# Weight sums of a seven-product matrix multiplication, formed in another order

## The chip, the core and the metric

The kernel runs on one core of one Trainium2 chip. The metric is device time in microseconds (us), from launch to end, taken as the median of several runs. The engines of a core run side by side, each in its own program order, and wait for one another through semaphores: PE is TensorE (its weight loads are listed as PEld), DVE is VectorE, ACT is ScalarE, POOL is GpSimd and SP is SyncE, which here issues the loads. A DMA that adds to its destination is issued on POOL.

## The reference

Two layers of a block over 528 tokens (16 meta tokens, 512 inputs) of width 1024, all in fp32. Each layer projects the normalized input with one wide matrix `w_in`, runs a sparse attention and a pooling branch, and mixes both under gates:

```
proj = jnp.einsum('btd,de->bte', h, w_in)
q, k, v, gate_a, u_b, gate_b, q_idx, k_idx, w_idx, merge = jnp.split(proj, ...)
...
attn = indexer_sparse_attention(q, k, v, q_idx, k_idx, w_idx, k_top)   # top 128 keys of a query
y_a = jnp.einsum('bte,ed->btd', attn * jax.nn.silu(gate_a), w_a)
y_b = jnp.einsum('bte,ed->btd', pooled * jax.nn.silu(gate_b), w_b)
g_a, g_b = jnp.split(jax.nn.sigmoid(merge), 2, axis=-1)
return x + jnp.einsum('btd,de->bte', g_a * y_a + g_b * y_b, w_out)
```

The change concerns the columns of `w_in` for `gate_a` (512) and `merge` (2048): ten chunks of 256 columns in each layer.

## The kernel before

**Precision.** A product in fp32 is made of three fast matmuls: each operand is split into a high part (a cast, on ACT) and a low part (operand less high part, on DVE), and high*high, high*low and low*high are added up in PSUM.

**Seven products.** For these ten chunks the 1024 x 256 weight block and the activations are cut into 2 x 2 quarters, and the four quarter results come from seven products instead of eight (Winograd's form of Strassen's method). A product is 12 matmuls of 128x128 weights on 264 columns in layer 0 and 256 in layer 1. The weight operands are the quarters a11, a12, a22 and four sums: s3 = a11 + a21, s1 = a21 + a22, s2 = s3 + a22, s4 = a12 + s2. The activations' sums are formed earlier, once in a layer.

**A group** (one round `q` of the loop in `mix_gates`) is the work of one chunk: seven products into three PSUM banks U, S and X. U gathers several products, and in between partial results are read out of it: `out` copies a bank on ACT (rows `p` and `u`), and `total` adds a bank and such a copy on DVE (rows `c<-d,p`, `c<-d,u`, and `sila<-d,p`, `sila<-d,u` in the first two groups of a layer). `gate` then takes a tanh on ACT. Banks change roles from group to group: the next group's U is this one's X, its X this one's S, its S this one's U. The order before is a11 into U, a12 into X, s2 into U, s1 into S, s3 into U, s4 into S, a22 into U.

**Where the weights come from.** A chunk's two `raw` tiles (four quarters in all) are loaded by SP, two chunks in flight; `w_load` asks for the next chunk once a chunk's last low part is taken. `mixed_prep` forms the operands in nine items, i0 to i8: casts on ACT (`hi`, L244), subtractions on DVE (`lo`, rows `w<-raw,w`), two sums on DVE (rows `s<-raw` and `raw<-s,raw`) and two sums by accumulating DMA issued on POOL (L253 for s1, L263 for s4). At each product's end the loop takes items so that some five of the next chunk's nine are done when its group begins; in the program's order i0 and i1 of the next chunk stand behind a group's fourth product, i2 behind the fifth, i3 and i4 behind the sixth and seventh, and the rest in its own group behind the first three. `NEEDS` says which item a product must have behind it.

**What runs beside it.** After each product `group_done` lets a step of the attention (`logits`, `soft`, `scale`, `turn`, `values`) be emitted, so that PE has matmuls of the attention between some products. In the first groups of a layer DVE also does the top-k rounds (`MAX8`, `MATCH_REPLACE8`). PE and DVE run in the order in which the program emits; the instructions of ACT, POOL and SP are placed by the framework's scheduler. PSUM has three `d` banks for U, S, X, four `a` banks and one `v` bank for the attention. POOL further scales the meta keys (`pm`, L765).

Of the kernel before, what the change touches and what calls it, by code (L numbers as in the profile page):

```python
# [8 lines left out]
F32 = mybir.dt.float32  # L9
F32R = mybir.dt.float32r  # L10
AF = mybir.ActivationFunctionType
OP = mybir.AluOpType
# [16 lines left out]
LB = 6  # L29
# [60 lines left out]
def tile_block(ctx: ExitStack, tc: tile.TileContext, x, meta, w_in, pool_w, w_a, w_b, w_out, rows, hgain, c_tab, out):  # L90
# [42 lines left out]
    raws, ready = {}, {}  # L133
# [37 lines left out]
    def w_prep_enqueue(casts_first=False, after=None):  # L171
        c = W["prep"]
        if c >= len(chunks):
            return
        W["prep"] += 1
        kt = chunks[c][0][0].shape[1]
        cols = 2048 // kt
        if c in plain:
            return
        ready[c] = {}  # L180
        if c in mixed:
            prep_q.extend(mixed_prep(c))
            return
        parts = ready[c] = ([], [])

        def split(which):
            t = w_tile().rearrange("p (k e) -> p k e", e=cols)
            parts[which].extend(t[:, k] for k in range(kt // 2))
            return t

        his = {}

        def high(s):
            his[s] = split(0)
            act.copy(his[s], raws[c][s])

        def low(s):
            dve.tensor_sub(split(1), raws[c][s], f(his[s]))
            if s == 1:
                del raws[c]  # L200
                w_load()

        def second():
            low(0)
            high(1)

        def minus(s):
            t = split(1)
            act.activation(t, raws[c][s], AF.Copy, scale=-1.0)  # L209
            gp.dma_start(t, raws[c][s], accum_op=OP.add)  # L210

        def plus(s):
            t = split(0)
            act.copy(t, raws[c][s])
            if s == 1:
                del raws[c]
                w_load()

        def highs():
            with tc.issue_after(after) if after else nullcontext():  # L220
                high(0)
                high(1)

        if casts_first:
            prep_q.extend((highs, lambda: low(0), lambda: low(1)))
        elif c in by_dma:
            prep_q.extend((lambda: minus(0), lambda: minus(1), lambda: plus(0)))
            if c in metas:
                prep_q.append(lambda: meta_queries(metas[c], raws[c]))
            prep_q.append(lambda: plus(1))  # L230
        else:
            prep_q.extend((lambda: high(0), second, lambda: low(1)))

    def mixed_prep(c):

        r0, r1 = raws[c]
        blk = {"a11": r0[:, 0], "a21": r0[:, 1], "a12": r1[:, 0], "a22": r1[:, 1]}
        src = {"a11": "a11", "a12": "a12", "a22": "a22", "s3": "s3", "s2": "a11", "s1": "a21", "s4": "a12"}
        ops = ready[c]

        def hi(n):
            t = w_tile().rearrange("p (s k e) -> p s k e", s=2, k=4)
            ops[n] = t
            act.copy(t[:, 0], blk[src[n]])  # L244

        def lo(n):
            dve.tensor_sub(ops[n][:, 1], blk[src[n]], f(ops[n][:, 0]))

        def i0():
            blk["s3"] = tmp.tile([128, 544], F32, tag="L", name="s3", bufs=LB)[:, :512].rearrange(  # L250
                "p (k e) -> p k e", k=4)
            dve.tensor_add(blk["s3"], blk["a11"], blk["a21"])
            gp.dma_start(blk["a21"], blk["a22"], accum_op=OP.add)  # L253
            hi("a11")

        def i1():
            lo("a11")
            dve.tensor_add(blk["a11"], blk["s3"], blk["a22"])
            hi("a12")

        def i2():
            lo("a12")
            gp.dma_start(blk["a12"], blk["a11"], accum_op=OP.add)  # L263

        def i3():
            hi("s2")

        def i4():
            lo("s2")
            hi("s1")  # L270

        def i5():
            lo("s1")
            hi("s3")

        def i6():
            lo("s3")
            hi("s4")

        def i7():  # L280
            lo("s4")
            hi("a22")

        def i8():
            lo("a22")
            del raws[c]
            w_load()

        def counted(fn):
            def item():  # L290
                fn()
                progress[c] += 1
            return item

        progress[c] = 0
        return [counted(fn) for fn in (i0, i1, i2, i3, i4, i5, i6, i7, i8)]
# [643 lines left out]
        return early, late, last_sum, operands  # L940

    ROLES = [(0, 1, 2), (2, 0, 1), (1, 2, 0)]
    NEEDS = {"a11": 1, "a12": 2, "s2": 4, "s1": 5, "s3": 6, "s4": 7, "a22": 8}

    def mix_gates(sa, zb, ta, s0, n2, operands, splits, alos):
        base = popped[0] - progress[W["use"]]
        for q in range(-2, 8):
            c = W["use"]
            W["use"] += 1
            ops = ready[c]  # L950
            w_prep_enqueue()
            bs = [bank("d") for _ in range(3)]
            U, S, X = (bs[r] for r in ROLES[(q + 2) % 3])
            done = [0]

            def product(ps, name, start):
                while progress[c] <= NEEDS[name]:
                    prep_one()
                B, wt = operands[name], ops[name]
                for k in range(4):  # L960
                    for e, (x, y) in enumerate(((0, 0), (0, 1), (1, 0))):
                        pe.matmul(ps[:, :n2], wt[:, x, k], B(y, k), start=start and k == e == 0,
                                  stop=k == 3 and e == 2, skip_group_check=True)

            def end():
                done[0] += 1
                group_done()
                while prep_q and (popped[0] < base + 9 * (q + 2) + LEAD + done[0] * 9 // 7 or (q == 7 and done[0] > 4)):
                    prep_one()

            def gate(eh, t, src, in_sheet):
                j = 2 * q + eh
                sign = -1.0 if eh else 1.0
                cs = slice(s0 + t * n2, s0 + (t + 1) * n2)
                if q < 0:
                    th = sheet(n2, "th")[:, :n2]
                    act.activation(th, src, AF.Tanh, scale=0.5)
                    d = sa[:, j + 4, cs]
                    later(lambda: dve.scalar_tensor_tensor(d, th, sign, src, op0=OP.add, op1=OP.mult),
                          3 if in_sheet else 2)  # L980
                elif q < 4:
                    th = src if in_sheet else sheet(n2, "th")[:, :n2]
                    act.activation(th, src, AF.Tanh, scale=0.5 * sign)
                    d = zb[:, j, cs]
                    later(lambda: dve.scalar_tensor_tensor(d, th, 1.0, d, op0=OP.add, op1=OP.mult), 2)
                else:
                    act.activation(ta[j - KT][:, cs], src, AF.Tanh, scale=0.5 * sign)

            def total(eh, t, ps, part):
                cs = slice(s0 + t * n2, s0 + (t + 1) * n2)  # L990
                o = sa[:, 2 * q + eh + 4, cs] if q < 0 else sheet(n2, "c")[:, :n2]
                dve.tensor_tensor(o, ps[:, :n2], part, op=OP.add)
                gate(eh, t, o, True)

            def out(ps, name):
                o = sheet(n2, name)[:, :n2]
                act.copy(o, ps[:, :n2])  # L997
                return o

            if q >= 4:  # L1000
                for j in (2 * q - KT, 2 * q + 1 - KT):
                    ta[j] = tmp.tile([128, T], F32, tag="B", name="ta", bufs=8)
            product(U, "a11", True)
            p1 = out(U, "p1")
            end()
            product(X, "a12", True)
            end()
            product(U, "s2", False)
            u = out(U, "u2")
            total(0, 0, X, p1)  # L1010
            end()
            product(S, "s1", True)
            p5 = out(S, "p5")
            end()
            if q == 7:
                alos()
            product(U, "s3", False)
            total(1, 1, U, p5)
            end()
            product(S, "s4", False)  # L1020
            end()
            product(U, "a22", False)
            total(0, 1, S, u)
            gate(1, 0, U[:, :n2], False)
            end()
            splits()
            ready.pop(c)
            if q == -1:
                later(lambda: SIL.update(ready=True), 4)
# [388 lines left out]
```

## Time and profile before

| what | value |
|---|---|
| median of 3 runs | 764.48 us (764.06 to 765.5) |
| profiled execution | 762.6 us |
| its span, first to last instruction | 760.7 us |
| PE busy | 738.2 us |
| DVE busy | 569.7 us |
| ACT busy | 474.9 us |
| POOL busy | 238.4 us |

The profiled execution is a run of its own, 1.9 us under the median; about 1.9 us of it lie outside the span. A row of the timeline reads: start in us from the span's start, duration, engine, line, operation, output<-inputs, shapes, count, and in brackets the engine's idle time before it and what ended it. All calls through the `Metered` wrapper, so all of PE's and DVE's, carry its line, L61; they are told apart by their tiles. A row of the waits reads: engine, what waited, what it waited for, us in total, times, longest. Where a group of rows is summed, the busy time and the mean duration in ns stand behind the bar, then the idle time before them. Matmuls are pipelined, so the end of a row overlaps the start of the next.

### The profile page before, as it was taken

The numbers are of one execution on the slowest core, as the hardware profiler recorded it, in microseconds if no ns is written. First come the engines' busy times: TensorE is split into PE (matmuls) and PEld (weight loads), VectorE is DVE, ScalarE is ACT, GpSimd is POOL, SyncE is SP. The second block draws the span as 40 slices with busy tenths as digits, with TensorE's granted clock in tenths as the row PEclk, the third lists the DMA queues.
The fourth block names the chain that finished last, engine by engine and source line by source line (L and its number), as shares of the span: only waits on it lengthen the run. The fifth ranks groups of instructions, "written<-read, shape, count | busy, mean of one in ns | idle before, by whom it ended". The sixth has DMA issues, their size and how long they took to land.

```text
span 760.7 us, 15982 instructions
## 1 busy us (share of the span) xinstructions
PE 738.2 (97%) x5962; PEld 708.9 (93%) x5962; DVE 569.7 (75%) x1436; ACT 474.9 (62%) x1077; POOL 238.4 (31%) x312
## 2 busy tenths in 40 slices
PE   8999999998999899999999999999999999999998
PEld 7999998998898899999998989998789999999998
DVE  6866998999886775794448668999989777658531
ACT  6669645656786887543245796557468778864320
POOL 3741075611122121063347411754023231205200
PEclk9999999999999999999999999999999999999999
DMA  7767755934454345443422676669255545346411
GB/s 259 226 166 169 167 126 123 239 99 99 113 124 97 92 103 126 140 161 134 141 85 84 165 180 175 165 155 228 41 141 115 128 94 125 85 130 206 139 43 42
DMA packets 99277, 103.26 MB, mean 136 GB/s; under 512 B 4816, under 2 KB 80368, under 8 KB 99200
## 3 DMA queue, kind: packets, MB, share of 16 engines
q1 hardware_dynamic: 88752, 74.89, 32.2%
q0 software_dynamic: 10368, 27.27, 19.4%
q8 instruction: 47, 0.77, 0.4%
q14 instruction: 30, 0.25, 0.1%
q10 hardware_dynamic: 80, 0.08, 0.0%
HBM read 66.41 MB, written 8.55 MB: 99 GB/s over the span
## 4 chain that ended last, share of the span: by engine, by line
PE 62%; DVE 19%; ACT 9%; DMA 6%; issue 3%; POOL 1%; DVEq 0%; SPq 0%; ACTq 0%; POOLq 0%
PE d L61 52%; PE a L61 8%; DMA raw<-raw 5%; DVE sc L61 4%; DVE m L61 3%; DVE w L61 3%; ACT w L244 3%; ACT lt L753 2%; DVE t L61 2%; PE v L61 2%; DVE qs L61 1%; ACT lt L764 1%; DVE ss L61 1%; DMA xt<-in_x_dram 1%; ACT pt L780 1%
## 5 line engine op out<-in xcount | busy, mean ns | idle before, releaser
L61 PE MATMUL d<-hhi,w 128*128 128x256 f32 (+3 forms) x1344 | 268.8, 292 | 0.5 <-DVE sila L61 0.3
L61 PEld LDWEIGHTS d<-hhi,w 128*128 128x128 f32 x1344 | 214.8, 189 | 3.8 <-issue 0.6
L61 PE MATMUL d<-hlo,w 128*128 128x256 f32 (+3 forms) x672 | 183.2, 289 | 0.0
L61 PEld LDWEIGHTS d<-hlo,w 128*128 128x128 f32 x672 | 126.8, 189 | 1.4 <-issue 0.2
L61 DVE TENSOR_TENSOR w<-raw,w 128x512 fp32r<-128x512 f32 (+1 forms) x152 | 124.5, 829 | 4.0 <-ACT w L244 3.9
L61 PE MATMUL d<-w,hhi 128*128 128x256 f32 x768 | 122.4, 288 | 0.8 <-DVE w L61 0.5
L61 PEld LDWEIGHTS d<-w,hhi 128*128 128x128 f32 x768 | 104.5, 189 | 5.2 <-issue 1.3
L61 PE MATMUL d<-hsum,w 128*128 128x264 f32 (+1 forms) x720 | 98.5, 289 | 7.8 <-ACT p L997 4.5
L61 PEld LDWEIGHTS d<-hsum,w 128*128 128x128 f32 x720 | 91.0, 191 | 10.4 <-ACT p L997 5.7
L244 ACT CAST w<-raw 128x512 fp32r<-128x512 f32 x120 | 70.8, 620 | 40.8 <-DVE raw L61 20.9
L61 PE MATMUL d<-w,hlo 128*128 128x256 f32 x384 | 72.3, 281 | 0.0
L61 PEld LDWEIGHTS d<-w,hlo 128*128 128x128 f32 x384 | 57.0, 188 | 0.0
L765 POOL TENSOR_SCALAR pm<-lt,rs 128x16 f32<-128x16 f32 x48 | 24.6, 558 | 98.3 <-DVE rs L61 89.0
L61 DVE MATCH_REPLACE8 sc<-m,sc 128x400 f32<-128x400 f32 (+2 forms) x100 | 54.3, 548 | 0.0
L61 DVE MAX8 m<-sc 128x8 f32<-128x400 f32 (+2 forms) x100 | 52.7, 556 | 0.9
L210 POOL DMA_DIRECT2D w<-raw x32 | 29.5, 940 | 72.5 <-ACT w L209 50.0
L61 PE MATMUL d<-mhi,w 128*128 128x272 f32 (+2 forms) x192 | 45.3, 324 | 0.0
L61 DVE SCALAR_TENSOR_TENSOR sc<-r,wsg,sc 128x144 f32<-128x144 f32 (+3 forms) x56 | 32.3, 581 | 16.1 <-ACT r L677 13.6
L753 ACT ACTIVATE lt<-lt,mn,NR 128x144 f32<-128x144 f32 (+3 forms) x64 | 42.3, 663 | 2.0 <-DVE mn L61 1.6
L253 POOL DMA_DIRECT2D raw<-raw x20 | 17.8, 889 | 79.3 <-DVE s L61 74.9
L1279 POOL TENSOR_TENSOR hlo<-ta,hhi 128x256 fp32r<-128x256 f32 (+1 forms) x28 | 28.3, 1021 | 43.3 <-PE d L61 30.5
L640 POOL TENSOR_TENSOR t<-t,t 128x256 f32<-128x256 f32 (+1 forms) x34 | 30.8, 907 | 26.8 <-DVE t L61 26.5
(215 smaller groups left out, 1442.4 us busy)
## 6 DMA issues: line engine op xcount, KB each, us to landing
raw<-in_w_in_dram SPq DMA_DIRECT2D x88, 256.0 KB, 3.1
raw<-in_w_in_dram SPq DMA_DIRECT2D x32, 512.0 KB, 4.6
w<-raw POOLq DMA_DIRECT2D x32, 512.0 KB, 5.3
raw<-raw POOLq DMA_DIRECT2D x40, 256.0 KB, 3.2
raw<-in_w_out_dram SPq DMA_DIRECT2D x16, 512.0 KB, 3.4
kept<-res SPq DMA_DIRECT2D x16, 264.0 KB, 4.8
res<-kept SPq DMA_DIRECT2D x16, 264.0 KB, 5.5
raw<-in_w_branch_b_dram SPq DMA_DIRECT2D x8, 512.0 KB, 5.0
```

Source lines behind the costliest of these rows:

```text
L61: return fn(*a, **k)
L210: gp.dma_start(t, raws[c][s], accum_op=OP.add)
L244: act.copy(t[:, 0], blk[src[n]])
L253: gp.dma_start(blk["a21"], blk["a22"], accum_op=OP.add)
L640: gp.tensor_tensor(t1[:m, :256], t1[:m, :256], t2[:m, :256], op=OP.add)
L753: act.activation(L[hh][:, :n], L[hh][:, :n], AF.Exp, scale=NR[:, i, h:h + 1], bias=mn[:, hh:hh + 1], accum_out=sm[:, hh:hh + 1])
L764: act.activation(L[hh][:, 16:n], L[hh][:, 16:n], AF.Copy, scale=rs[:, hh:hh + 1])
L765: (gp if j < 3 else dve).tensor_scalar(pms[i][:, 2 * j + hh, :], L[hh][:, 0:16], rs[:, hh:hh + 1], None, op0=OP.mult)
L780: act.copy(pt[:, :2 * len(bs)], tp[:, :256 * len(bs)].rearrange("p (a c) -> p a c", c=128))
L1279: pool_end = gp.tensor_sub(hlo[:, j, a:a + n], d, f(hhi[:, j, a:a + n]))
```

## The change

The sums are formed otherwise. s3 = a21 + a11 is now made by the accumulating DMA, in a21's place, by `first_sum`, which is called half a group ahead: in item i4 of the chunk before (for a layer's first chunk, at the end of the preparation before it). s2 = s3 + a22 is made on DVE in item i1, in a tile of its own. s4 = a12 + s2 stays a DMA in item i2. s1 = s2 - a11 is made on DVE, in a11's place, also in item i2. The last two products change places: a22 into U now comes right behind s3 into U, and s4 into S is the last; their operands are prepared in that order too, and the tanh of U stands behind a22, ahead of s4.

```diff
             if s == 1:
                 del raws[c]
                 w_load()
+                first_sum(c + 1)
...
+    def first_sum(c):
+        if c in mixed:
+            gp.dma_start(raws[c][0][:, 1], raws[c][0][:, 0], accum_op=OP.add)
+
...
-        src = {"a11": "a11", "a12": "a12", "a22": "a22", "s3": "s3", "s2": "a11", "s1": "a21", "s4": "a12"}
+        src = {"a11": "a11", "a12": "a12", "a22": "a22", "s3": "a21", "s2": "s2", "s1": "a11", "s4": "a12"}
...
         def i0():
-            blk["s3"] = tmp.tile([128, 544], F32, tag="L", name="s3", bufs=LB)[:, :512].rearrange(
-                "p (k e) -> p k e", k=4)
-            dve.tensor_add(blk["s3"], blk["a11"], blk["a21"])
-            gp.dma_start(blk["a21"], blk["a22"], accum_op=OP.add)
             hi("a11")
 
         def i1():
             lo("a11")
-            dve.tensor_add(blk["a11"], blk["s3"], blk["a22"])
+            blk["s2"] = tmp.tile([128, 544], F32, tag="L", name="s2", bufs=LB)[:, :512].rearrange(
+                "p (k e) -> p k e", k=4)
+            dve.tensor_add(blk["s2"], blk["a21"], blk["a22"])
             hi("a12")
 
         def i2():
             lo("a12")
-            gp.dma_start(blk["a12"], blk["a11"], accum_op=OP.add)
+            gp.dma_start(blk["a12"], blk["s2"], accum_op=OP.add)
+            dve.tensor_sub(blk["a11"], blk["s2"], blk["a11"])
...
         def i4():
             lo("s2")
             hi("s1")
+            first_sum(c + 1)
...
         def i6():
             lo("s3")
+            hi("a22")
+
+        def i7():
+            lo("a22")
             hi("s4")
 
-        def i7():
+        def i8():
             lo("s4")
-            hi("a22")
-
-        def i8():
-            lo("a22")
             del raws[c]
             w_load()
...
-    NEEDS = {"a11": 1, "a12": 2, "s2": 4, "s1": 5, "s3": 6, "s4": 7, "a22": 8}
+    NEEDS = {"a11": 1, "a12": 2, "s2": 4, "s1": 5, "s3": 6, "a22": 7, "s4": 8}
...
             product(U, "s3", False)
             total(1, 1, U, p5)
             end()
+            product(U, "a22", False)
+            gate(1, 0, U[:, :n2], False)
+            end()
             product(S, "s4", False)
-            end()
-            product(U, "a22", False)
             total(0, 1, S, u)
-            gate(1, 0, U[:, :n2], False)
             end()
```

## The prediction

> **What bounds the kernel now.** I read the page's first part and its chain, then the busy time by stretch over the two stages that the change touches, then who waited for whom, then single rows around the places where the new order bites.
>
> ```profile
> span 760.7 us, 15982 instructions
> PE 738.2 (97%) x5962; PEld 708.9 (93%) x5962; DVE 569.7 (75%) x1436; ACT 474.9 (62%) x1077; POOL 238.4 (31%) x312
> PE d L61 52%; PE a L61 8%; DMA raw<-raw 5%; DVE sc L61 4%; DVE m L61 3%; DVE w L61 3%; ACT w L244 3%; ACT lt L753 2%; DVE t L61 2%; PE v L61 2%; DVE qs L61 1%; ACT lt L764 1%; DVE ss L61 1%; DMA xt<-in_x_dram 1%; ACT pt L780 1%
> ```
>
> TensorE works 97% of the span. The chain also runs through `DMA raw<-raw`, the two accumulating transfers per group that the change moves: 5% of 760.7 us, some 38 us. Being on the chain is not yet time to be won: what TensorE can win is its idle time. The next view cuts the two mixing stages (ten groups of seven products in each layer) into five stretches: groups 1-3, 4-6 and 7-10 of layer 0, groups 11-12 and 13-20 of layer 1. The columns are length, busy time of PE, weight load, DVE, ACT and POOL, clock, DMA share, GB/s.
>
> ```profile
> 168.00:213.00 45.00, 41.43 (x340) 39.81 (x339) 41.05 (x118) 30.77 (x85) 7.80 (x14) 1.00 0.46 106
> 213.00:263.00 50.00, 45.04 (x381) 43.05 (x380) 35.62 (x99) 38.97 (x99) 11.19 (x17) 1.00 0.44 101
> 263.00:320.00 57.00, 56.66 (x511) 55.18 (x510) 38.96 (x98) 43.14 (x98) 7.95 (x12) 1.00 0.44 111
> 543.00:572.00 29.00, 26.01 (x196) 24.78 (x195) 26.11 (x74) 18.57 (x51) 4.97 (x9) 0.94 0.47 109
> 572.00:686.00 114.00, 113.54 (x1013) 110.25 (x1011) 84.19 (x228) 92.08 (x221) 24.39 (x35) 1.00 0.48 117
> ```
>
> PE's idle time is length less busy: 3.57, 4.96, 0.34, 2.99 and 0.46 us, together 12.3 us. That is the most that better-placed weight sums can bring. Groups 7-10 and 13-20 have almost none: there every wait put on PE lengthens the kernel. Who held PE and ACT:
>
> ```profile
> PE d L61 <- ACT p L997: 4.7, 5, 2.8
> PE d L61 <- DVE w L61: 3.3, 5, 1.5
> PE a L61 <- ACT lt L764: 1.9, 3, 1.2
> PE a L61 <- ACT pt L780: 1.4, 1, 1.4
> ACT w L244 <- DVE raw L61: 20.9, 20, 3.4
> ACT w L244 <- DMA raw<-raw: 19.3, 17, 3.7
> ```
>
> ACT waits 19.3 us for the accumulating DMAs in 17 places, in order, with the copies that PE needs (`p`) queued behind. One instance, in groups 5 and 6, is the largest PE wait of all:
>
> ```profile
> 237.82 0.89 POOL L253 DMA_DIRECT2D raw<-raw  x1
> 239.94 0.68 DVE L61 TENSOR_TENSOR w<-raw,w 128x512 fp32r<-128x512 f32 x1
> 242.83 0.62 ACT L244 CAST w<-raw 128x512 fp32r<-128x512 f32 x1 [3.68 <-DMA raw<-raw]
> 248.66 0.38 ACT L997 COPY p<-d 128x264 f32<-128x264 f32 x1
> 249.09 1.12 PE L61 MATMUL d<-hsum,w 128*128 128x264 f32 x7 [2.77 <-ACT p L997]
> ```
>
> The s1 sum is issued on POOL at 237.82 and lands just before ACT resumes at 242.83; ACT has stood for 3.68 us, works off its backlog, and reaches `p` at 248.66, and PE has stood for 2.77 us.
>
> **The change, part by part.** *Amount of work.* It removes one 128x512 DVE add per group (`s<-raw`) and puts a subtraction in (s1 = s2 - a11), so two DVE operations and two accumulating DMAs per group stay:
>
> ```profile
> L61 DVE TENSOR_TENSOR s<-raw 128x512 f32<-128x512 f32 x20 | 13.6, 680 | 0.0
> L61 DVE TENSOR_TENSOR raw<-s,raw 128x512 f32<-128x512 f32 x20 | 13.8, 692 | 0.7
> raw<-raw POOLq DMA_DIRECT2D x40, 256.0 KB, 3.2
> ```
>
> The sum of work is nil: 20 x 0.68 us leaves the DVE queue at one place and 20 x 0.69 us enters at another, and 40 transfers of 256 KB stay 40. What counts is position.
>
> *The new wait.* Products write three PSUM banks U, S, X. Before, s3 added into U, then DVE read U (`total(1,1)`), PE meanwhile did s4 into S, and only then a22 went into U. Now a22 follows s3 at once, into the bank that DVE is still reading: PE has to wait for `total(1,1)`. Before, that read was covered by the s4 product. The before trace shows the very wait once, where DVE was late (group 2; first s3, then s4, then the first matmul of a22):
>
> ```profile
> 192.14 1.49 PE L61 MATMUL d<-hsum,w 128*128 128x264 f32 x11
> 193.46 0.28 PE L61 MATMUL d<-hhi,w 128*128 128x264 f32 x1
> 195.37 0.39 PE L61 MATMUL d<-hhi,w 128*128 128x264 f32 x1 [0.30 <-DVE sila L61]
> 194.29 0.68 DVE L61 TENSOR_TENSOR s<-raw 128x512 f32<-128x512 f32 x1
> 194.89 0.43 DVE L61 TENSOR_TENSOR sila<-d,p 128x264 f32<-128x264 f32 x1
> ```
>
> DVE's read ends at 194.89 + 0.43 = 195.32 (the rows are rounded), and a22 starts at 195.37, 0.05 to 0.06 us later. The Trainium skill's page "PSUM — Partial Sum Buffer", section "PSUM bank collisions raise a hardware error", says that accesses of a bank by two engines must be ordered by bank and partition quadrant, not by address; by that the wait cannot be escaped by columns, and the 195.37 row agrees. Where DVE is idle the price is the floor seen in group 17:
>
> ```profile
> 635.30 1.58 PE L61 MATMUL d<-hsum,w 128*128 128x256 f32 x12
> 636.73 0.28 PE L61 MATMUL d<-hhi,w 128*128 128x256 f32 x1
> 637.00 0.42 DVE L61 TENSOR_TENSOR c<-d,p 128x256 f32<-128x256 f32 x1 [2.65 <-PE d L61]
> ```
>
> s3 ends at 636.88, DVE reads from 637.00 to 637.42, a22 could start at 637.48, while PE started its next product at 636.73: 0.75 us. Where DVE is late it costs more; where attention matmuls lie between the two products, nothing (group 5):
>
> ```profile
> 236.01 1.97 PE L61 MATMUL v<-pt,V 128*64 128x128 f32 x32
> 236.75 0.42 DVE L61 TENSOR_TENSOR c<-d,p 128x264 f32<-128x264 f32 x1
> 238.82 0.37 PE L61 MATMUL d<-hhi,w 128*128 128x264 f32 x1
> ```
>
> The read is over at 237.17, long before 238.82. The order of instructions on PE is the same in both kernels, so these fillers stay where they are. DVE's order is eased by one thing: before, the `s<-raw` add stood directly ahead of `total(1,1)` in most groups (194.29 above); now the add comes behind it. So I move DVE's read 0.68 us forward, but not ahead of s3's end + 0.12, and do not move it in groups 10 and 20, where no mixed chunk follows. The first and the last of the twenty:
>
> ```profile
> 180.73 0.28 PE L61 MATMUL d<-hhi,w 128*128 128x264 f32 x1
> 181.36 0.43 DVE L61 TENSOR_TENSOR sila<-d,p 128x264 f32<-128x264 f32 x1
> 682.15 0.28 PE L61 MATMUL d<-hhi,w 128*128 128x256 f32 x1
> 682.75 0.42 DVE L61 TENSOR_TENSOR c<-d,p 128x256 f32<-128x256 f32 x1
> ```
>
> Group 1: 181.36 + 0.43 + 0.06 - 180.73 = 1.12 as it stands, 0.75 with the add gone. Group 20: 682.75 + 0.42 + 0.06 - 682.15 = 1.08. Read this way, groups 1-3 give 0.75, 1.24, 0.14; groups 4-6 0.76, 0, 0; groups 7-10 0, 0, 0.76, 1.18; groups 11-12 0.34, 0.80; groups 13-20 0.79, 0.41, 0.47, 0.75, 0.76, 0, 0.76, 1.09. Sum 11.0 us; without the eased DVE 14.3 us.
>
> *What goes.* The s3 sum is issued half a group ahead and waits only for a weight load; the s4 transfer is used an item later; ACT's s1 cast now follows a DVE subtraction instead of a landing. In the instance of groups 5 and 6 that subtraction can stand right behind the row at 239.94: about 240.6 + 0.7 = 241.3 against 242.83, so 1.5 us of ACT's 3.68 go, up to 2.2 with the add gone ahead of it. The built order also puts the softmax exponentials ahead of that cast on ACT, so they no longer queue behind it. It is not all gain: in about half of the groups DVE reaches that place after the transfer used to land.
>
> *The other moves.* `total(0,1)` now waits for the last product of the group; the gated sums behind it on DVE then start at most one product (1.5 us) later, and its bank is wanted again only after the next group's a11 product, so I cost it at nothing; if DVE is late as well, the cover shrinks and costs up to the 0.43 us of the read itself per group. The first sum on POOL stands behind `pm` and in front of the next `pm`; both wait long already, so nothing, or up to a 3.2 us transfer where a weight load is late.
>
> **The sum by stretch.** Groups 1-3: new waits 2.13, DVE-bound (41.05 of 45), PE idle 3.57 already, so most of the new wait takes the place of idle time; ends 0 and +2.1, I take +0.8. Groups 4-6: +0.76, and of 4.96 idle I credit 3.8, since the two big waits hang on ACT's DMA waits: -3.0 (ends -4.2 and +0.8). Groups 7-10: +1.9, no idle to win. Groups 11-12: +1.14, of 2.99 I credit 1.9, as part of it is ACT's: -0.8 (ends -1.9 and +1.1). Groups 13-20: +5.0, of 0.46 idle perhaps 0.1: +4.9. Sum 0.8 - 3.0 + 1.9 - 0.8 + 4.9 = +3.8 us. The profiled execution takes 762.6 us (span 760.7), 1.9 under the median of 764.48: 762.6 + 3.8 = 766.4 for it, and 768.3 for the median.
>
> **The rivals.** *Faster.* In groups 13-20 PE may only look full: the transfers are on the chain (38 us of it), and if the loop transfer, ACT, PE, DVE sets the pace there, then an opened loop lets PE run ahead and the new waits fall into slack. Price: 0 - 4.2 + 1.9 - 1.9 + 1.0 = -3.2, so 761.3. It decides from the point where under about 1 us of the 5.0 shows in groups 13-20. Against it: 0.46 us idle in 114. The Trainium skill's page "DMA: Bandwidth & Descriptors", section "Rules for kernel authors", is on this side: issue a transfer early and wait for it late, so that its fixed cost overlaps. The 3.68 us row agrees that the late one hurts. Chance 0.17. *No change:* gains of about 8 us against losses near 9: 764.5, chance 0.15. *Much slower:* ACT's s1 cast merely waits for DVE, no idle is won, and DVE is no earlier: +12, up to +14.3, so 776.5 to 778.8; chance 0.10. *The first sum is not early:* POOL is in order and DVE's s2 add then waits for the transfer: 3.2 us in a few groups on top of the forecast, some 774; chance 0.04. The forecast, between 1.5 and 8 us slower, has 0.54.
>
> **The numbers.** 0.2% is 1.5 us, about what a measurement of this kernel can tell from none. Faster 0.17, within 0.15, slower 0.54 + 0.10 + 0.04 = 0.68. The range reaches into the faster rival at -2.5 and past the forecast to +9.5: 762.0 to 774.0.
>
> **What would show it.** Right: in some 14 of 20 groups a PE wait of 0.5 to 1.2 us at the first a22 matmul, released by DVE's `c` or `sila`, about 10 us in all; ACT's waits for `raw<-raw` near nothing; the 2.77 us wait at group 6 below 1. Wrong: PE idle in groups 13-20 staying under 1.5 us, or the waits for `p` and `lt` staying as they are.

## The result, and the profile after

The changed kernel takes 767.86 us (median of 7 runs, 765.79 to 771.51) against 763.94 us (7 runs, 761.51 to 765.5): a ratio of 1.0064, 95% interval 1.0036 to 1.0093. It is slower, by 4 to 5 us; the forecast was 768.3. That the time came out this close is partly luck: two steps of the sum were 3 to 5 us too pessimistic each, and one that was costed at nothing cost 8 us.

The page of the kernel after begins so (span, busy time and the chain's shares; then, from the list of transfers, the two kinds of accumulating DMA with their count, size and median time from issue to landing):

```profile
span 765.2 us, 15969 instructions
PE 739.8 (97%) x5962; PEld 711.4 (93%) x5962; DVE 568.5 (74%) x1436; ACT 476.6 (62%) x1077; POOL 238.1 (31%) x312
PE d L61 65%; PE a L61 10%; PE v L61 4%; DVE sc L61 2%; DVE m L61 2%; DVE w L61 2%; DVE t L61 1%; DMA w<-raw 1%; DMA raw<-s 1%; DVE qs L61 1%; DVE c L61 1%; ACT lt L758 1%; DVE ss L61 1%; DMA xt<-in_x_dram 0%; DVE nf L61 0%
...
raw<-raw POOLq DMA_DIRECT2D x20, 256.0 KB, 4.1
raw<-s POOLq DMA_DIRECT2D x20, 256.0 KB, 3.2
```

The profiled execution takes 767.03 us, 0.83 under its median. The chain has lost `DMA raw<-raw`, 5% before, and keeps 1% of `DMA raw<-s`, the s4 sum. The kernel is slower all the same: being on the chain was not time to be won. Who held PE and ACT after the change:

```profile
PE d L61 <- DVE c L61: 6.5, 10, 1.0
PE a L61 <- DVE qs L61: 5.5, 2, 5.4
PE d L61 <- DVE sila L61: 2.0, 4, 0.6
PE d L61 <- ACT p L1002: 0.8, 1, 0.8
ACT w L249 <- DVE s L61: 16.1, 18, 2.0
ACT w L249 <- DVE raw L61: 4.4, 7, 1.8
ACT w L249 <- DMA raw<-s: 1.6, 3, 0.7
```

Three things are to be seen. ACT's waits for accumulating DMAs fell from 19.3 us to 1.6, and no wait of PE for the copy `p` exceeds 0.8 us: the 2.77 us of group 6 are gone. The predicted new wait stands in 14 places, 6.5 + 2.0 = 8.5 us, released by `c` or `sila`. And there is a wait of 5.4 us, for `qs`, that the prediction does not have. A single instance of the new wait, in group 17 (a row of the timeline each):

```profile
638.57 0.28 PE L61 MATMUL d<-hsum,w 128*128 128x256 f32 x1
...
638.96 0.42 DVE L61 TENSOR_TENSOR c<-d,p 128x256 f32<-128x256 f32 x1 [4.26 <-PE d L61]
...
639.44 0.38 PE L61 MATMUL d<-hhi,w 128*128 128x256 f32 x1 [0.59 <-DVE c L61]
```

The last matmul of s3 ends at 638.85, DVE reads from 638.96 to 639.38, a22 starts at 639.44. PE shows 0.59 us of idle time; a following matmul would have started 0.16 us before the end of the one ahead (636.73 against 636.88 in the prediction's rows), so a place costs 0.75, the floor that was forecast. Fourteen places: 8.5 + 14 x 0.16 = 10.7 us.

The busy time by stretch, now with every stretch cut at a group's first matmul (length, busy time of PE, weight load, DVE, ACT and POOL, clock, DMA share, GB/s), first before, then after; the rows are groups 1-3, 4-6, 7-10, 11-12 and 13-20:

```profile
170.64:212.74 42.10, 38.53 (x316) 36.91 (x315) 38.15 (x112) 28.60 (x79) 6.95 (x13) 1.00 0.49 113
212.74:262.82 50.08, 45.12 (x382) 43.13 (x380) 35.70 (x98) 39.05 (x98) 11.19 (x17) 1.00 0.44 101
262.82:319.70 56.88, 56.84 (x513) 55.36 (x511) 38.84 (x99) 43.02 (x97) 7.95 (x12) 1.00 0.44 110
543.55:571.62 28.07, 25.08 (x190) 23.98 (x188) 25.18 (x69) 17.64 (x49) 4.18 (x8) 0.94 0.49 113
571.62:685.20 113.58, 113.24 (x1012) 110.16 (x1011) 83.77 (x230) 91.67 (x220) 24.77 (x35) 1.00 0.48 115
```

```profile
179.12:217.74 38.62, 37.43 (x315) 36.69 (x314) 36.03 (x107) 29.27 (x83) 7.86 (x13) 1.00 0.50 117
217.74:262.23 44.49, 43.89 (x381) 43.06 (x380) 34.04 (x94) 37.93 (x92) 12.73 (x17) 1.00 0.50 110
262.23:321.40 59.17, 57.56 (x515) 55.74 (x514) 39.62 (x102) 44.24 (x100) 7.18 (x11) 1.00 0.46 111
544.94:571.26 26.32, 23.36 (x189) 22.41 (x188) 25.27 (x70) 18.87 (x52) 5.62 (x10) 1.00 0.54 120
571.26:690.50 119.24, 114.25 (x1012) 110.29 (x1011) 85.00 (x231) 93.02 (x221) 21.00 (x34) 1.00 0.46 110
```

The lengths change by -3.5, -5.6, +2.3, -1.8 and +5.7: together -2.9 us. The twenty groups have become faster. The loss stands ahead of them: group 1 begins at 179.12 instead of 170.64, 8.5 us later. There the timeline after shows, at the rotation of the queries in layer 0:

```profile
140.18 3.50 SPq L148 DMA_DIRECT2D raw<-in_w_in_dram  x4
...
144.72 0.92 POOL L237 DMA_DIRECT2D raw<-raw  x1 [5.94 <-DMA raw<-in_w_in_dram]
145.38 1.02 POOL L645 TENSOR_TENSOR t<-t,t 128x256 f32<-128x256 f32 x1
...
146.44 0.41 DVE L61 TENSOR_TENSOR t<-a,Sg 16x256 f32<-16x256 f32 x1 [6.22 <-POOL t L645]
...
151.17 0.72 PE L61 MATMUL a<-identr,qs 128*128 128x128 f32 x4 [5.39 <-DVE qs L61]
```

Read it from the top. The first sum's turn on POOL (L237) comes at 144.72 - 5.94 = 138.78, before SP has even issued the load of the first mixed chunk's weights, at 140.18; POOL stands for 5.94 us until they have landed. Behind it in POOL's order is the add `t<-t,t` of the rotation; DVE waits for that 6.22 us, and PE, which needs `qs` from DVE, 5.39 us. And it does not end there:

```profile
150.00:152.00 2.00, 0.83 (x5) 0.86 (x6) 1.97 (x6) 1.16 (x3) 1.68 (x4) 0.51 0.00 0
152.00:154.00 2.00, 2.00 (x10) 2.00 (x10) 2.00 (x7) 2.00 (x5) 2.00 (x3) 0.50 0.96 193
154.00:156.00 2.00, 2.00 (x11) 2.00 (x10) 1.97 (x7) 1.38 (x3) 1.50 (x2) 0.50 0.85 168
156.00:158.00 2.00, 2.00 (x16) 1.85 (x15) 2.00 (x7) 0.86 (x4) 0.78 (x2) 0.78 1.02 169
```

After the idle time the granted clock is 0.50, and it is back at 1.00 only behind 157. From 152 to 158 that is 2 x (0.50 + 0.50 + 0.22) = 2.4 us of matmul time lost, on top of the 5.4.

### The profile page after: what moved, and what is told of

It reads as the page before. It is cut to its first block, busy times and chain, and to the rows that moved or that the text cites. A ratio compares the mean times of both kernels' runs of the same rounds, so it can differ in the third digit from the quotient of the medians.

```text
span 765.2 us, 15969 instructions
## 1 busy us (share of the span) xinstructions
PE 739.8 (97%) x5962; PEld 711.4 (93%) x5962; DVE 568.5 (74%) x1436; ACT 476.6 (62%) x1077; POOL 238.1 (31%) x312
## 4 chain that ended last, share of the span: by engine, by line
PE 78%; DVE 13%; DMA 3%; ACT 2%; issue 2%; POOL 1%; SPq 0%; DVEq 0%; POOLq 0%; ACTq 0%
PE d L61 65%; PE a L61 10%; PE v L61 4%; DVE sc L61 2%; DVE m L61 2%; DVE w L61 2%; DVE t L61 1%; DMA w<-raw 1%; DMA raw<-s 1%; DVE qs L61 1%; DVE c L61 1%; ACT lt L758 1%; DVE ss L61 1%; DMA xt<-in_x_dram 0%; DVE nf L61 0%
## 5 line engine op out<-in xcount | busy, mean ns | idle before, releaser
L61 PE MATMUL d<-hsum,w 128*128 128x264 f32 (+1 forms) x720 | 96.5, 286 | 2.2 <-DVE w L61 1.4
L237 POOL DMA_DIRECT2D raw<-raw x20 | 17.8, 891 | 95.7 <-DMA raw<-in_w_in_dram 31.6
L61 PE MATMUL d<-mhi,w 128*128 128x272 f32 (+2 forms) x192 | 47.4, 335 | 0.0
L266 POOL DMA_DIRECT2D raw<-s x20 | 17.4, 871 | 95.9 <-DVE w L61 43.5
```

Of the source, the lines that this page charges most:

```text
L61: return fn(*a, **k)
L237: gp.dma_start(raws[c][0][:, 1], raws[c][0][:, 0], accum_op=OP.add)
L266: gp.dma_start(blk["a12"], blk["s2"], accum_op=OP.add)
```

## Experiments

Two questions: what does each part of the change do, and where do the gains come from? The theories in the expectations: **A**, the new order makes PE wait and costs about what was forecast, against **B**, that the waits fall into slack. **C**, the first sum of a layer's first chunk holds POOL and with it PE, against **D**, that its 5.4 us are hidden or given back later. **E**, the gain of the new sums is that ACT's s1 cast no longer hangs on a transfer, against **F**, that it is the half group's lead of the first sum. **G**, the gain is that s4's cast comes an item later, against **H**, that the sums lie in other tiles. Ratios are to the kernel before, in runs on the same chip.

**The sums alone.** The changed kernel with the last two products in the order of before; the operands are still prepared a22 first.

```diff
-            product(U, "a22", False)
-            gate(1, 0, U[:, :n2], False)
-            end()
             product(S, "s4", False)
+            end()
+            product(U, "a22", False)
             total(0, 1, S, u)
+            gate(1, 0, U[:, :n2], False)
             end()
```

> The weight sums of the changed kernel, but the products in the order of before (s3, s4, a22). Theory A (the new order makes PE wait for DVE's read of U, 9.5 us in visible waits and 0.16 us each of overlap lost, 14 places): these waits vanish and PE-bound groups shorten by the same, about 11 us under the changed kernel, 755 to 759 us, so 5 to 9 us faster than before. Rival B (PE has slack there and the loop of transfers, ACT and DVE sets the pace): 764 to 767 us, the PE idle time turning up at other waits.

Measured: 760.99 us, ratio 0.9965 (0.9947 to 0.9984). This is faster than before, and lies between A's range and B's: undoing the order wins some 7 us, not 11 and not 3. By the traces it shortens groups 4-10 and 13-20 by 8.9 us against after; 1.2 of them go again in groups 11-12 (27.55 us against 26.32), where this execution has a clock of 0.94.

**The order alone.** The kernel before with the last two products exchanged, nothing else; the operands are still prepared s4 first.

> The kernel before with only the last two products exchanged (a22 right behind s3); sums as before. Theory A: the same PE waits for DVE's read of U as in the changed kernel or larger, as the add still stands ahead of that read on DVE: 11 to 14 us slower than before, 774 to 778 us. Rival B: at most 3 us slower, since in the kernel before ACT's waits for the transfers leave slack for it.

Measured: 768.88 us, ratio 1.0075 (1.0054 to 1.0097), +5.4 us by the medians. Its waits, and its groups 13-20, beside those of the sums alone (second fence):

```profile
PE d L61 <- DVE c L61: 7.4, 10, 1.3
PE d L61 <- DVE sila L61: 3.3, 4, 1.0
...
571.80:692.10 120.30, 114.55 (x1012) 110.43 (x1011) 85.49 (x231) 92.46 (x220) 22.01 (x35) 1.00 0.46 112
```

```profile
570.80:684.20 113.40, 112.74 (x1012) 110.09 (x1011) 84.19 (x233) 92.30 (x221) 23.27 (x34) 1.00 0.48 113
```

The order alone brings 14 waits of 10.7 us in all, and where PE is full they lengthen the kernel one for one: 120.30 us in place of 113.58 before, while the new sums with the old order take 113.40. So A's mechanism stands, and B falls where PE is full; but of 10.7 us of waits only 5.4 reach the end, and the time lies between the two ranges. Elsewhere the new waits replace others: those for `p` are down to 2.2 us from 4.7.

**The first chunk's sum on DVE.** The changed kernel; in a layer's first chunk s3 is added by DVE in item i0, in the same place, and no first sum is issued in the preparation before it.

```diff
                 del raws[c]
                 w_load()
-                first_sum(c + 1)
...
         def i0():
+            if c - 1 not in mixed:
+                dve.tensor_add(blk["a21"], blk["a21"], blk["a11"])
             hi("a11")
```

> The changed kernel, but the first sum of a layer's first chunk is made by DVE in place (0.68 us) instead of by a DMA on POOL. Theory C (that DMA waits on POOL for a weight load with the q rotation's add queued behind it; PE stands for 5.4 us before the stage and then runs at a lower clock for two dense products, 2.5 us): the stage of layer 0 begins 7 to 9 us earlier, and as groups 1 to 3 are then bound by DVE's top-k again, 3 to 4 us of it are lost there: 761 to 766 us. Rival D (DVE's top-k sets the time up to group 3, the PE wait is covered by it): 767 to 769 us, as the changed kernel.

Measured: 759.61 us, ratio 0.9955 (0.9936 to 0.9974). Two of twenty early sums undone, one per layer, and the kernel is 8.3 us faster than the full change (1.0064 - 0.9955 = 0.0109 of 763.5) and faster than before. C's mechanism stands, and is worth more than it was given, so the time lies below C's range: the 5.4 us of idle time and the 2.4 us of the clock make 7.8, and its mean granted clock is 1.000 where after has 0.993. Its stretches, the change without this hold-up on POOL (below: the block):

```profile
174.55:214.69 40.14, 37.94 (x315) 36.87 (x314) 37.77 (x111) 30.23 (x85) 7.84 (x13) 1.00 0.52 119
214.69:259.73 45.04, 44.37 (x381) 43.15 (x380) 35.29 (x97) 37.79 (x92) 12.19 (x17) 1.00 0.48 109
259.73:318.89 59.16, 57.55 (x515) 55.73 (x514) 39.62 (x102) 44.26 (x100) 7.17 (x11) 1.00 0.44 112
541.92:566.75 24.83, 23.24 (x189) 22.41 (x188) 23.74 (x67) 17.96 (x50) 5.49 (x9) 1.00 0.55 127
566.75:685.93 119.18, 114.33 (x1012) 110.36 (x1011) 85.95 (x233) 92.95 (x221) 21.75 (x34) 1.00 0.47 111
```

Against after, 1.5 us of the block are given back in groups 1-3 (38.62 against 40.14; C had 3 to 4), where DVE is the bound and had time to get ahead, and another 1.5 us appear in groups 11-12 (26.32 against 24.83). Nearly all of those are two waits of PE in group 11 after the change, 0.78 us for `p` and 1.40 us for a low part `w`, where without the block there is one of 0.66 us for `w`. What in layer 1 makes them longer is not shown.

**Both.** The new sums, the old order, and the first chunk's sum on DVE.

> Both: products in the order of before, and the first chunk's first sum on DVE; all other sums as in the changed kernel. Theories A and C together: 750 to 756 us, 8 to 14 us faster than before. If B holds: 760 to 765 us. If A and D hold: as the run with the sums alone, 755 to 759 us.

Measured: 753.18 us, ratio 0.9857 (0.9839 to 0.9875): the fastest kernel here, together with "no early sum" below, and 10.3 us better than before, as A and C together had it. The order costs 6.4 us here too (759.61 - 753.18), the block 7.8 (760.99 - 753.18): the parts add up. So the change is -10.3 for the sums, +5.4 to +6.9 for the order, about +8 for the block, some +4 in all.

**s1 off the transfer.** The kernel before; only s1 = a21 + a22 is added on DVE, behind s4's transfer.

```diff
         def i0():
             ...
-            gp.dma_start(blk["a21"], blk["a22"], accum_op=OP.add)
             hi("a11")
...
             gp.dma_start(blk["a12"], blk["a11"], accum_op=OP.add)
+            dve.tensor_add(blk["a21"], blk["a21"], blk["a22"])
```

> The kernel before, with one of its two transfers gone: s1 = a21 + a22 is added on DVE in item i2 instead of by DMA on POOL; s3 and s2 stay on DVE, s4 stays a transfer, products in the order of before. It has 20 more DVE operations of 0.69 us (13.8 us). Theory E (the gain of the changed sums, 10 us, came from taking ACT's s1 cast off a transfer issued too late, so that PE no longer stands for ACT): nearly all of it is seen here too, less what the DVE-bound groups 1 to 3 and 11 to 12 pay for 5 more operations (0.7 us each): 755 to 759 us. Rival F (the gain came from the s3 add leaving DVE's queue and from the early transfer): no gain, 763 to 768 us.

Measured: 760.7 us, ratio 0.996 (0.9942 to 0.9978), 2 to 3 us of the 10. Neither E's range nor F's.

**No early sum at all.** The kernel "both", with s3 on DVE in place in every chunk and no first sum by DMA.

> The best version so far (changed sums, products in the order of before, first chunk's s3 on DVE), but s3 of every chunk is added on DVE, in place, so that no first sum is issued on POOL at all: what the early transfer itself brings. 18 more DVE operations of 0.68 us than in that version. Theory E: 2 to 4 us slower than it, 755 to 758 us. Rival F: 8 to 12 us slower than it, 761 to 766 us.

Measured: 753.91 us, ratio 0.9866 (0.9846 to 0.9886). The interval overlaps that of "both": issuing the sum half a group ahead brings nothing that these runs can tell from none, although DVE does eighteen adds more. F falls; the time is also just below E's range, which had charged 2 to 4 us for those adds. The Trainium skill's page "DMA: Bandwidth & Descriptors", section "Rules for kernel authors", which stood behind the rival "faster", advises issuing early and waiting late; here the early issue by itself brought nothing, and in front of a queue that others need it cost 8 us.

**The change once more**, in further runs, since so much hangs on the block.

> The changed kernel once more, on the chip of the two others, for the comparison: 766 to 770 us; the wait of over 5 us on PE for the q rotation near 150 us is there again if it belongs to the kernel, and is not if it was a chance of one execution.

Measured: 767.85 us, ratio 1.0071 (1.004 to 1.0101). Its waits show the same one for `qs`, longer still:

```profile
PE a L61 <- DVE qs L61: 6.7, 1, 6.7
```

**s4 prepared last, and s4 prepared early.** The first is "s1 off the transfer" with the operands prepared a22 before s4; the second is "no early sum" with them prepared s4 before a22. The order of the products is that of before in both.

```diff
         def i6():
             lo("s3")
-            hi("s4")
+            hi("a22")
 
         def i7():
-            lo("s4")
-            hi("a22")
+            lo("a22")
+            hi("s4")
 
         def i8():
-            lo("a22")
+            lo("s4")
...
-    NEEDS = {"a11": 1, "a12": 2, "s2": 4, "s1": 5, "s3": 6, "s4": 7, "a22": 8}
+    NEEDS = {"a11": 1, "a12": 2, "s2": 4, "s1": 5, "s3": 6, "a22": 7, "s4": 8}
```

> The version with s1 added on DVE and everything else as before (760.7 us), but with the operands a22 and s4 prepared in the other order (a22's cast and subtraction first, s4's last, in items i6 to i8); products in the order of before. Theory G (what is left of the gain is that s4, the operand that a transfer forms, is cast one item later, so ACT never waits for it): 753 to 756 us, as the version with s3 in place. Rival H (it is the tile: s3 lies in a tile of its own from i0 to i6 and holds one of six that the softmax needs too, against s2's from i1 to i4): 759 to 762 us.

> The version with all s3 on DVE in place (753.9 us), but with s4 prepared ahead of a22, as before. Theory G: it loses what s4's later cast had brought, 758 to 762 us. Rival H: 753 to 755 us, no change.

Measured: 756.41 us, ratio 0.9909 (0.9881 to 0.9937), and 756.55, ratio 0.9906 (0.9882 to 0.9931). Both land between the two theories' ranges, which fits each of G and H holding in part. By the ratios, s1 off the transfer is worth 0.4%, s4 an item later 0.4 to 0.5% (0.9906 to 0.9866 and 0.9960 to 0.9909), and the other place of s3 and s2 0.4 to 0.5% (0.9909 to 0.9866 and 0.9960 to 0.9906); the steps down to 0.9866 rest on intervals that just overlap (its own ends at 0.9886, theirs begin at 0.9881 and 0.9882). ACT's wait for s4's transfer shows G's half: first with s4 early, then in "no early sum", with s4 an item later.

```profile
ACT w L248 <- DMA raw<-s: 6.4, 8, 2.2
```

```profile
ACT w L248 <- DMA raw<-s: 2.4, 3, 1.3
```

Why the other place of s3 and s2 brings something is open: s3 in a21's place and s2 in a tile of its own change how long that tile is held and which operation ACT waits for, and no run separates the two.

## Why the prediction came out right

Step by step, in us; the second column is the first chunk's sum on DVE, so the change without the block, against before:

| stretch | predicted | without the block | after |
|---|---|---|---|
| groups 1-3 | +0.8 | -2.0 | -3.5 |
| groups 4-6 | -3.0 | -5.0 | -5.6 |
| groups 7-10 | +1.9 | +2.3 | +2.3 |
| groups 11-12 | -0.8 | -3.2 | -1.8 |
| groups 13-20 | +4.9 | +5.6 | +5.7 |
| sum | +3.8 | -2.3 | -2.9 |
| elsewhere, by the medians | 0 | about -1.5 | about +7 |

The last row is the difference of the medians (-3.8 and +3.9) less the sum: single executions of one kernel differ by 4 us (before: 761.51 to 765.5), so the block's worth is not read from where group 1 starts. Counted from one row that all three have, the add `RQ<-RQ` on POOL (at 129.61 before, 133.54 without the block, 130.33 after), group 1 begins 41.03, 41.01 and 48.79 us later: the block is 7.8 us in the traces as well, and the 3.9 us by which the execution without the block is late at that row come from ahead of it.

**The new wait, right where PE is full.** The floor of 0.75 us, 14 places, the releasers `c` and `sila`, some 10 us in all: all there. In groups 13-20 PE's idle time is now 119.24 - 114.25 = 4.99 us, and the stretch is 5.7 longer, the 0.16 us of lost overlap at each place included. Since `total` reads the same columns of U that a22 adds to, the rows show the wait, but not whether other columns of the bank would escape it.

**The new wait, over-priced where DVE is the bound.** In groups 1-3 and 11-12, 2.13 + 1.14 us were charged. Order against old order, with the sums the same ("first chunk's sum on DVE" against "both"), the lengths there are 40.14 against 40.41 and 24.83 against 24.94: nothing at all. The whole wait took the place of idle time, not "most of" it; the order costs 7.8 us by these two traces' stretches, 5.4 to 6.9 by the medians, and not 11.

**The gains, under-priced.** The steps credited 7.1 us of PE's idle time; "both" against before has -1.7, -5.7, 0.0, -3.1 and +0.4, some 10:

```profile
172.13:212.54 40.41, 38.15 (x316) 36.88 (x315) 38.08 (x111) 30.34 (x84) 8.12 (x13) 1.00 0.52 118
212.54:256.88 44.34, 44.03 (x381) 43.01 (x380) 35.58 (x100) 37.74 (x93) 12.25 (x17) 1.00 0.49 109
256.88:313.78 56.90, 56.90 (x513) 55.39 (x511) 38.20 (x98) 43.29 (x97) 6.95 (x11) 1.00 0.44 111
537.67:562.61 24.94, 23.11 (x189) 22.34 (x188) 23.60 (x66) 17.12 (x47) 4.71 (x7) 1.00 0.55 127
562.61:676.60 113.99, 113.05 (x1012) 110.19 (x1011) 85.32 (x235) 92.36 (x222) 21.98 (x34) 1.00 0.47 112
```

In groups 4-6, 0.3 us of idle time are left of 5.0, where 3.8 were credited. In groups 11-12 the gain exceeds the idle time (3.1 against 2.99), which "the most that better-placed weight sums can bring" rules out: that step took idle time for all there is to win, though its own row showed a clock of 0.94. Of the 3.1 us, 1.2 are idle time (2.99 down to 1.83) and 2.0 are busy time (25.08 down to 23.11). In the kernel before, two waits there come shortly after one another, and the clock falls:

```profile
564.20 0.62 PE L61 MATMUL a<-consts,lt 128*128 128x128 f32 x2 [1.22 <-ACT lt L764]
565.26 2.93 PE L61 MATMUL d<-hsum,w 128*128 128x256 f32 x12 [0.45 <-ACT u L997]
...
564.00:566.00 2.00, 1.36 (x5) 1.02 (x6) 1.97 (x6) 2.00 (x8) 0.00 (x0) 0.82 0.70 208
566.00:568.00 2.00, 2.00 (x12) 2.00 (x11) 0.71 (x2) 1.03 (x5) 0.89 (x1) 0.50 0.96 254
```

A product of 12 matmuls takes 2.93 us. In "both" the second wait is gone, the first is 1.16 us, the clock stays at 1.00, and the product takes 1.69:

```profile
557.25 0.62 PE L61 MATMUL a<-consts,lt 128*128 128x128 f32 x2 [1.16 <-ACT lt L770]
557.80 1.69 PE L61 MATMUL d<-hsum,w 128*128 128x256 f32 x12
```

**The first sum on POOL, missed.** "Behind `pm` and in front of the next `pm` ... so nothing, or up to a 3.2 us transfer where a weight load is late" is the step that failed. It looked at POOL's neighbours inside the groups only; a layer's first chunk has its first sum in the preparation before it, and there the neighbour is the rotation's add, which DVE and PE wait for. The price is not the transfer either but the wait for its source: 5.94 us, and the clock behind it. The rival "the first sum is not early" named POOL's order, but placed the harm at DVE's s2 add, priced it at 3.2 us in a few groups and gave it 0.04.

So the total was right because some 6 us by the stretches, 7.6 by the medians, of under-priced gains and over-priced waits stood against some 8 of a block that was missed.

## What to carry to other kernels

When a DMA is issued earlier on an engine's in-order queue, look up for its very first issue what that engine does for others at that point, and when the transfer's source lands; a wait there is passed on to all that stand behind it. Price a new wait in full only in stretches where the waiting engine has no idle time, and at nothing where another engine is the bound. A rearranged sum of parts is worth taking apart: here two of three parts lost what the third won, and the version without them takes 753.18 us.

## What was not expected of the hardware

Idle time of PE can cost more than itself. After 5.4 us without matmuls the granted clock was 0.50 for some 6 us, 2.4 us more; and two waits of 1.22 and 0.45 us, their ends 1.06 us apart, were followed by 0.50 as well, while the single one of 2.77 us in group 6 was not (the stretch of groups 4-6 before has a clock of 1.00).

The length of the waits alone does not decide it. In group 11 PE waits 0.8 us for `p` and then 1.40 us for a low part `w`, the ends 1.9 us apart, both after the change and in the run with the sums alone. The stretches behind the second wait (it ends at 551.06 after, and at 549.38 with the sums alone), first after, then the sums alone:

```profile
552.00:556.00 4.00, 3.80 (x34) 3.65 (x32) 3.97 (x13) 2.10 (x8) 0.00 (x0) 1.00 0.62 140
```

```profile
550.00:554.00 4.00, 4.00 (x25) 4.00 (x25) 3.86 (x12) 1.86 (x7) 0.00 (x0) 0.64 0.50 133
```

After the change the clock stays at 1.00; with the sums alone it falls, and the 34 matmuls behind the wait take 5.81 us instead of 4.29. The Trainium skill's page "TensorE: Matmul & The Clock Gate", Part 1, says that a half-rate clock follows an idle window of about 3.4 us; the wait of 5.4 us agrees, the drop after 1.22 and 0.45 us does not by length alone. The page calls the window free-running, so the place of a wait in it may decide; the two executions of group 11 fit that, but no run here moves a wait on purpose.

Early transfers were also slower: the first sum took 4.1 us from issue to landing at the median, the s4 sum 3.2. What slows it was not measured.
